# Hybrid attention, RG-LRU and PEER block on one core: more up products ahead, and every second down product in two float32r parts

## Chip, core and metric

One core of one Trainium2 chip runs the whole program. The metric is device time in microseconds, the median of several runs. TensorE (PE) multiplies, VectorE (DVE), ScalarE (ACT) and GpSimd (POOL) work on tiles in on-chip memory, SyncE (SP) issues most transfers; GpSimd issues the gathers by index.

## What is computed

512 tokens of width 1024 go through one layer: RMSNorm, one projection that feeds differential attention (8 heads, block-causal) and an RG-LRU branch, a gated merge, an output projection, and then a PEER layer, which is what the change is about. PEER picks for each token, in each of 8 heads, 16 of 16384 experts by product keys, that is 128 experts a token, and adds up

```
u = u_tab[idx]                                  # (token, head, 16, 1024)
act = gelu(einsum('thkd,td->thk', u, hb))
wts = softmax(top_s) * act
out = einsum('thk,thkd->td', wts, v_tab[idx])
```

All in float32.

## The kernel before, in words

Token blocks are numbered 0 to 3, 128 tokens each. A first pass (`p0`) takes block 0 through attention, RG-LRU and merge, a second pass (`p1`) blocks 1 to 3, its matmuls in two float32r parts (a value is a high part and a rest, and a product is three matmuls: high by high, high by low, low by high; helper `mm`, lines 206 to 211). PEER is done in two ways. For blocks 0 and 1 `experts` gathers the 128 picked rows of u and v of each token (1 MB for one slot of 128 tokens, an indirect DMA on GpSimd's queue) and VectorE does two passes over each: a dot product (line 855) and an accumulation into x1 (line 838). For blocks 2 and 3 (256 tokens) the work is dense: all 16384 experts, in 128 chunks of 128.

The dense part of a chunk c is an *up* product (tokens by the chunk's 128 rows of u, 8 accumulated products of 256 columns into PSUM, then gelu to an output y), a weight table (how much each token wants each expert), and a *down* product (y times table gives o; o times the chunk's rows of v is accumulated over all chunks in PSUM tile `acc`, 4 products of 512 columns).

Stages, in order of time, after the second pass's key products (`p1.keys`, whose last matmul is at 940 us):

1. Top-k on VectorE for blocks 1 to 3. Beside it, `ups_far` runs `LEAD` = 26 up products ("far", PSUM tile `pup`).
2. `wbuild`, 16 groups of 16 tokens: the table is built by one-hot products (PSUM tile `pw`) from one-hots that VectorE, ScalarE and GpSimd make, and is stored to DRAM (`w_d`) group by group; tiles of 12 chunks of it are loaded back (`wload`), the last two groups' rows only after the last store. 13 more up products (`up_near`, PSUM tile `st`) belong to this stage, seven of them written inside the loop, six after it.
3. The loop over c from 0 to 127: `down(c)` for all, and from c = `HEAD` = 24 on one `up_near` a step until all 128 are made. The order `TURN` makes chunks 24 to 38 first, then 0 to 23, then 39 to 127.

The first `AHEAD` = 39 up products use plain float32 (the token side is tile `h2r`, one load of 512 KB of u each into one of three buffers `raw`). The 89 others split u into two float32r parts (`chunk`: ScalarE casts, line 899, VectorE subtracts, line 900) and take the token side from `h2T`, which the second pass's projection has left in two parts for all three blocks. The down product is plain float32: two instructions for each product. Tiles of v hold two chunks (1 MB).

A planner in the compiler simulates the program and fixes each engine's order and SyncE's order from it, mostly by the order of writing where several things are ready; a tile with n buffers makes the next user wait for the n-th last. Gathers are paced by hand: each step adds a share (`SHARE`: 0.2 for a far up, 0.5 for a group of the table, 0.6 for a down step, 1.1 for a step with both) and one expert slot is issued for each whole one, tied behind an instruction of that step. `trunk` holds pools of the attention part, which are given back after the second pass's projection; `mid` takes their place.

Of the kernel before, what the change touches and what calls it, by code (L numbers as in the profile page):

```python
# [9 lines left out]
F32 = mybir.dt.float32  # L10
F32R = mybir.dt.float32r
# [4 lines left out]
ALU = mybir.AluOpType  # L16
# [46 lines left out]
def block_kernel(  # L63
# [25 lines left out]
    pp = ctx.enter_context(tc.tile_pool(name="pp", bufs=2))  # L89
    dram = ctx.enter_context(tc.tile_pool(name="dram", bufs=1, space=bass.MemoryType.DRAM))  # L90
    wp = ctx.enter_context(tc.tile_pool(name="wp", bufs=4))
    ap = ctx.enter_context(tc.tile_pool(name="ap", bufs=1))
    rg = ctx.enter_context(tc.tile_pool(name="rg", bufs=5))
    trunk = ctx.enter_context(ExitStack())
    s4 = trunk.enter_context(tc.tile_pool(name="s4", bufs=2, side="right"))
    s2 = trunk.enter_context(tc.tile_pool(name="s2", bufs=5, side="right"))

# [107 lines left out]

    def mm(o, lhs, rhs, start, stop):
        terms = [(0, 0)] if len(lhs) == 1 or len(rhs) == 1 else [(0, 0), (0, 1), (1, 0)]
        for i, (a, b) in enumerate(terms):
            nc.tensor.matmul(  # L209
                o, lhs[a], rhs[b], start=start and i == 0, stop=stop and i == len(terms) - 1  # L210
            )


    in_turn = mybir.DependencyInfo(mybir.DependencyClass.Sync, mybir.DependencyReason.SCHED_ONLY)
# [597 lines left out]
    def run(*gens):  # L812
        gens = list(gens)
        while gens:
            for g_ in list(gens):
                try:
                    next(g_)
                except StopIteration:
                    gens.remove(g_)
# [60 lines left out]
    NG = NT2 // TG  # L880
    NCH = SLOTS

    HEAD, MID = 24, 15
    AHEAD = HEAD + MID

    TURN = list(range(HEAD, AHEAD)) + list(range(HEAD)) + list(range(AHEAD, SLOTS))

    LEAD = 26

    WI = 12  # L890

# [9 lines left out]
        return t[:, 0, :], t[:, 1, :]  # L901


    def up(c, S_):
        ks = lambda k: slice(k * P, (k + 1) * P)
        if c < AHEAD:
            u = wp.tile([P, D], F32, tag="raw", name=nm("u"), bufs=3)
            nc.sync.dma_start(u, u_t[c])
            for k in range(KT):
                mm(S_, [u[:, ks(k)]], [p1.h2r[:, k, :]], k == 0, k == KT - 1)  # L910
        else:
            uhi, ulo = chunk(u_t, c, "near")
            for k in range(KT):
                mm(S_, [uhi[:, ks(k)], ulo[:, ks(k)]], [h[:, k, P : 3 * P] for h in p1.h2T], k == 0, k == KT - 1)

    def gelu(o, S_):
        return A.activation(o, S_, AF.Gelu_apprx_tanh)  # L917
# [26 lines left out]


    def kept(c):
        if c >= HEAD:
            return mid.tile([P, NT2], F32, tag="ym", name=nm("y"), bufs=MID)
        if c % WI == 0:
            ybuf.append(rg.tile([P, WI, NT2], F32, tag="r", name=nm("ys")))  # L950
        return ybuf[-1][:, c % WI, :]
# [11 lines left out]

    def dense(ys, kT, kTb, stack):
        pool = lambda n, bufs=1, **kw: stack.enter_context(tc.tile_pool(name=n, bufs=bufs, reuse_waits="tile", **kw))
        dw = pool("dw")
        pa = pool("pa", space=PSUM)
        pt_ = pool("pt", 2, space=PSUM)
        acc = pa.tile([P, 2, D], F32, tag="acc", name="acc")

        def up_near():
            c = TURN[len(ys)]
            st = pt_.tile([P, 512], F32, tag="st", name=nm("st"))
            up(c, st[:, 0:NT2])
            y = kept(c)
            gelu(y, st[:, 0:NT2])
            ys[c] = y


        def wbuild(tg):  # L980
            o1s = wp.tile([P, TG, P], F32, tag="w8", name=nm("o1s"))
            st = wp.tile([P, NCH, TG], F32, tag="w8", name=nm("wst"))
            for t4 in range(0, TG, 4):
                pw = pt_.tile([P, 4, P], F32, tag="pw", name=nm("pw"))
                t0_ = tg * TG + t4
                o2 = dw.tile([P, 4, P], F32, tag="o2", name=nm("o2"), bufs=4)
                V.tensor_tensor(  # L987
                    o2, iota.unsqueeze(1).to_broadcast([P, 4, P]),
                    kTb[:, t0_ : t0_ + 4].unsqueeze(2).to_broadcast([P, 4, P]), op=ALU.is_equal,
                )  # L990
                for j in range(4):
                    t = t0_ + j
                    o1 = o1s[:, t4 + j, :]
                    k1, g1 = kT[:, 0, 0, t : t + 1], kT[:, 0, 1, t : t + 1]
                    if O1[j] == "A":

                        sq = dw.tile([P, P], F32, tag="osq", name=nm("osq"), bufs=2)
                        A.activation(sq, iota, AF.Square, bias=kT[:, 1, 0, t : t + 1])
                        A.activation(o1, sq, AF.Relu, scale=kT[:, 1, 1, t : t + 1], bias=g1)
                    else:  # L1000
                        e = nc.gpsimd if O1[j] == "P" else V
                        e.tensor_scalar(o1, iota, k1, g1, op0=ALU.is_equal, op1=ALU.mult)  # L1002
                    nc.tensor.matmul(pw[:, j, :], o2[:, j, :], o1, start=True, stop=True)  # L1003
                turn[0] = A.copy(st[:, :, t4 : t4 + 4], pw.rearrange("p t i -> p i t"))  # L1004
            nc.sync.dma_start(w_d[tg], st)

        ws, vs = [], []

# [9 lines left out]
        def down(c, y):  # L1018
            if c % WI == 0 and len(ws) * WI < NCH:
                wtile()  # L1020
                wload(len(ws) - 1)
            if c % 2 == 0:
                vs.append(wp.tile([P, 2, D], F32, tag="w8", name=nm("v")))
                nc.sync.dma_start(vs[-1], v_t[c : c + 2].rearrange("c p d -> p c d"))
            v_ = vs[-1][:, c % 2, :]
            o = mid.tile([P, NT2], F32, tag="o", name=nm("o"), bufs=OB)
            yv = y.rearrange("p (g t) -> p g t", g=NG)
            turn[0] = V.tensor_mul(o.rearrange("p (g t) -> p g t", g=NG), yv, ws[c // WI][:, :, c % WI, :])  # L1028
            for b in range(2):
                bs = slice(b * P, (b + 1) * P)  # L1030
                for hf in range(2):
                    hs = slice(hf * 512, hf * 512 + 512)
                    mm(acc[:, b, hs], [o[:, bs]], [v_[:, hs]], c == 0, c == NCH - 1)

        for tg in range(NG):
            wbuild(tg)
            share("w")
            if len(ys) < AHEAD - 6:
                up_near()

            if tg == 7:
                wtile()
                wload(0, 0, 8)
            elif tg == 13:
                wload(0, 8, 14)
        wload(0, 14, NG)
        while len(ys) < AHEAD:
            up_near()
        for c in range(NCH):
            down(c, ys[c])  # L1050
            if c >= HEAD and len(ys) < NCH:
# [20 lines left out]
    p1.rnn()  # L1072
    p1.merge()
    p1.project()
    trunk.close()
    mid = ctx.enter_context(tc.tile_pool(name="mid", bufs=1, reuse_waits="tile", side="right"))
    run(p1.keys())
    when = []
    for name, mark in marks:
        owed[0] += PACE[name]  # L1080
# [7 lines left out]
    def second():  # L1088
        x1 = cpool.tile([P, D], F32, tag="x1f", name="x1g")
        h2 = cpool.tile([P, D], F32, tag="h2f", name="h2g")  # L1090
        nc.sync.dma_start(x1, x1_d[0])
        nc.sync.dma_start(h2, h2_d)
        yield from experts(P, x1, h2, (p1.idx[:, 0, :], p1.g[:, 0, :]), lambda s: turn[0], True)

    ex = second()
    ys = ups_far(0, LEAD)
    p1.weights()
    kTs = picks_t()
# [86 lines left out]
```

## Time and profile before

| | us |
|---|---|
| median of 3 runs | 1912.57 |
| lowest, highest | 1909.86, 1913.16 |
| profiled execution | 1909.11 |
| its span | 1907.2 |
| PE, DVE, ACT, POOL busy | 1750.3, 1310.4, 783.9, 486.7 |
| up products, far (`pup`): first to last start | 940.5 to 1031.4 |
| one-hot products (`pw`): first to last start | 1051.9 to 1180.0 |
| down products (`acc`): first to last start | 1199.9 to 1900.0 |

Busy time of an engine counts its compute instructions. "Matmul" rows count machine instructions: a plain float32 product is two, a product of two-part operands three, a plain float32r one. Matmuls overlap at their ends, so the time of one is read best from a long chain of them.

### The profile page before, as it was taken

To read this page: it belongs to the slowest core of one execution; us is meant where nothing else is said; L and a number is where in the kernel's file an instruction comes from. 1 tells how busy PE (TensorE), PEld (TensorE's weight loads), DVE (VectorE), ACT (ScalarE), POOL (GpSimd) and SP (SyncE) were. 2 spreads that over 40 slices of the span, in tenths; PEclk is the share of its full clock that TensorE was granted. 3 is DMA by queue.
4 is the path that set the end of the run, shared out by engine and by line. 5 is a ranking of instruction groups with operands and counts; after the bars stand their busy time and mean duration, and the time that the engine had idled before them with its cause. 6 is when DMAs were issued, how large, how long until landed. Compare 5 with 4: busy or idle time off the path is not lost.

```text
span 1907.2 us, 25762 instructions
## 1 busy us (share of the span) xinstructions
PE 1750.3 (92%) x9166; PEld 1378.6 (72%) x9166; DVE 1310.4 (69%) x2818; ACT 783.9 (41%) x2193; POOL 486.7 (26%) x375
## 2 busy tenths in 40 slices
PE   7899898888798899989996985899999999999998
PEld 6789797778598677779985885347766767667763
DVE  2251387988889987689999567456666666666662
ACT  3382333767678754355311565012222322232220
POOL 1100001545322233342001466122222232222220
PEclk9899897889599899999998998899999999999999
DMA  7488454887877899987464577999999999999893
GB/s 296 149 279 309 172 193 162 297 293 283 308 274 278 313 389 357 386 305 271 155 216 157 177 275 290 362 372 395 366 369 392 382 354 364 354 356 354 331 359 123
DMA packets 131471, 563.37 MB, mean 295 GB/s; under 512 B 11408, under 2 KB 43280, under 8 KB 88592
## 3 DMA queue, kind: packets, MB, share of 16 engines
q1 hardware_dynamic: 94480, 293.29, 42.8%
q0 software_dynamic: 36864, 268.45, 37.0%
q8 instruction: 72, 1.18, 0.2%
q14 instruction: 55, 0.45, 0.1%
HBM read 539.68 MB, written 22.02 MB: 295 GB/s over the span
## 4 chain that ended last, share of the span: by engine, by line
PE 71%; DVE 11%; DMA 9%; ACT 5%; issue 3%; POOL 1%; DVEq 0%; SPq 0%; ACTq 0%; POOLq 0%
PE acc L209 22%; PE st L209 16%; DMA uv<-in_uv_dram,idx 6%; PE ppq L209 5%; PE pkq L209 5%; PE pgt L209 4%; PE pbR L684 4%; PE pbA L677 3%; PE pwo L711 2%; DVE x1f L838 2%; PE pw L1003 2%; PE pvv L209 1%; DMA w_d<-wst 1%; DVE uv L855 1%; DMA v<-in_v_t_dram 1%
## 5 line engine op out<-in xcount | busy, mean ns | idle before, releaser
L848 POOL DMA_INDIRECT uv<-in_uv_dram,idx x256 | 360.4, 1408 | 1075.8 <-DVE x1g L838 284.3
L209 PE MATMUL acc<-v,o 128*128 128x512 f32 x1024 | 449.9, 595 | 22.2 <-DVE o L1028 19.6
L209 PEld LDWEIGHTS acc<-v,o 128*128 128x128 f32 x1024 | 191.8, 191 | 246.5 <-issue 223.3
L209 PE MATMUL st<-a,t 128*128 128x256 f32 x2136 | 282.2, 292 | 0.0
L209 PEld LDWEIGHTS st<-a,t 128*128 128x128 f32 x2136 | 262.5, 191 | 22.2 <-issue 18.9
L838 DVE SCALAR_TENSOR_TENSOR x1g<-uv,e,x1g 128x1024 f32<-128x1024 f32 x128 | 164.3, 1283 | 52.8 <-ACT e L861 52.8
L838 DVE SCALAR_TENSOR_TENSOR x1f<-uv,e,x1f 128x1024 f32<-128x1024 f32 x128 | 164.0, 1281 | 24.9 <-ACT e L870 24.8
L855 DVE SCALAR_TENSOR_TENSOR uv<-uv,h2f 128x1024 f32<-128x1024 f32 x128 | 156.0, 1220 | 34.5 <-DMA uv<-in_uv_dram,idx 27.9
L855 DVE SCALAR_TENSOR_TENSOR uv<-uv,h2g 128x1024 f32<-128x1024 f32 x128 | 155.9, 1218 | 19.4 <-DMA uv<-in_uv_dram,idx 19.4
L860 ACT ACTIVATE e<-e 128x1 f32<-128x1 f32 x128 | 25.8, 202 | 333.7 <-DVE uv L855 333.4
L900 DVE TENSOR_TENSOR t<-raw,t 128x1024 fp32r<-128x1024 f32 x89 | 108.9, 1223 | 68.7 <-ACT t L899 68.7
L1028 DVE TENSOR_TENSOR o<-y,w 128x256 f32<-128x256 f32 x104 | 44.0, 424 | 102.9 <-PE acc L209 102.9
L917 ACT ACTIVATE y<-st 128x256 f32<-128x256 f32 x89 | 34.2, 384 | 193.5 <-PE st L209 193.5
L230 DVE TENSOR_TENSOR wl<-raw,wh 128x1024 fp32r<-128x1024 f32 x76 | 90.8, 1218 | 19.0 <-ACT wh L229 7.3
L899 ACT CAST t<-raw 128x1024 fp32r<-128x1024 f32 x89 | 92.0, 1033 | 23.4 <-PE acc L209 23.4
L229 ACT CAST wh<-raw 128x1024 fp32r<-128x1024 f32 x76 | 76.7, 1046 | 35.0 <-PE pwo L711 12.3
L209 PE MATMUL pup<-r,u 128*128 128x256 f32 x416 | 90.4, 379 | 0.1
L209 PEld LDWEIGHTS pup<-r,u 128*128 128x128 f32 x416 | 78.8, 190 | 11.1 <-issue 0.5
L1003 PE MATMUL pw<-o1s,o 128*128 128x128 f32 x512 | 70.8, 295 | 15.0 <-DVE o L987 9.8
L1002 POOL TENSOR_SCALAR o1s<-iota,r 128x128 f32<-128x128 bf16 x64 | 74.2, 1168 | 38.3 <-ACT r L928 16.3
L1003 PEld LDWEIGHTS pw<-o1s,o 128*128 128x128 f32 x512 | 66.6, 206 | 20.0 <-ACT wst L1004 9.0
L209 PE MATMUL pkq<-wh,a 128*128 128x256 f32 x384 | 78.5, 298 | 0.0
(264 smaller groups left out, 3251.1 us busy)
## 6 DMA issues: line engine op xcount, KB each, us to landing
v<-in_v_t_dram SPq DMA_DIRECT2D x64, 1024.0 KB
raw<-in_u_t_dram SPq DMA_DIRECT2D x89, 512.0 KB
u<-in_u_t_dram SPq DMA_DIRECT2D x39, 512.0 KB
w<-in_w_br_dram SPq DMA_DIRECT2D x16, 1024.0 KB
w_d<-wst SPq DMA_DIRECT2D x16, 1024.0 KB
w<-w_d SPq DMA_DIRECT2D x9, 1536.0 KB
w<-in_w_qkv_dram SPq DMA_DIRECT2D x12, 1024.0 KB
raw<-in_w_qkv_dram SPq DMA_DIRECT2D x24, 512.0 KB
```

What stands on the lines that cost most here:

```text
L209: nc.tensor.matmul(o, lhs[a], rhs[b], start=start and i == 0, stop=stop and i == len(terms) - 1)
L229: A.copy(hi[:, i : i + 1024], raw)
L230: V.tensor_tensor(lo[:, i : i + 1024], raw, hi[:, i : i + 1024].bitcast(F32), op=ALU.subtract)
L677: nc.tensor.matmul(pb[:, 0:NT], w.raw(k * P, (k + 1) * P), self.aT[:, k, :], start=(k == 0), stop=(k == H - 1))
L684: nc.tensor.matmul(pb[:, 0:NT], w.raw(1024 + k * P, 1024 + (k + 1) * P), self.rnn_out(k, 1)[:, 0, :], start=(k == 0), stop=(k == NF - 1),)
L838: V.scalar_tensor_tensor(x1, v_, e_, x1, op0=ALU.mult, op1=ALU.add)
L848: i = nc.gpsimd.indirect_dma_start(out=t, out_offset=None, in_=uv, in_offset=bass.IndirectOffsetOnAxis(ap=idx[:, s : s + 1], axis=0),)
L855: i = V.scalar_tensor_tensor(t[:, 0:D], t[:, 0:D], 1.0, h2, op0=ALU.mult, op1=ALU.mult, accum_out=d)
L899: A.copy(t[:, 0, :], raw)
L900: V.tensor_tensor(t[:, 1, :], raw, t[:, 0, :].bitcast(F32), op=ALU.subtract)
L1002: e.tensor_scalar(o1, iota, k1, g1, op0=ALU.is_equal, op1=ALU.mult)
L1003: nc.tensor.matmul(pw[:, j, :], o2[:, j, :], o1, start=True, stop=True)
```

## The change

- `AHEAD` goes from 39 to 47 (8 more, in a new tile `spare`) and `LEAD` from 26 to 31: 31 far ups, 10 inside the build loop, and 6 after it (`HELD`). Those 6 get a dependency for order alone: the first matmul of each comes behind the last one-hot product.
- 81 up products are left for the loop over c. They take the token side from `h2s`, two float32r tiles made once from `h2r`.
- Every odd chunk's down product is done in two parts: v and o are each cast on ScalarE to float32r, the rest is a subtraction on VectorE, and `mm` makes three matmuls of each product. The parts' pool `sp` has one buffer a tile; it lies where the pool `dw` of the table build was.
- Pool `ap` (which holds `h2T`) moves into `trunk`, and `trunk` is closed after `p1.keys` rather than before.

```diff
--- before.py
+++ after.py
@@ -89,9 +89,9 @@
     pp = ctx.enter_context(tc.tile_pool(name="pp", bufs=2))
     dram = ctx.enter_context(tc.tile_pool(name="dram", bufs=1, space=bass.MemoryType.DRAM))
     wp = ctx.enter_context(tc.tile_pool(name="wp", bufs=4))
-    ap = ctx.enter_context(tc.tile_pool(name="ap", bufs=1))
     rg = ctx.enter_context(tc.tile_pool(name="rg", bufs=5))
     trunk = ctx.enter_context(ExitStack())
+    ap = trunk.enter_context(tc.tile_pool(name="ap", bufs=1, side="right"))
     s4 = trunk.enter_context(tc.tile_pool(name="s4", bufs=2, side="right"))
     s2 = trunk.enter_context(tc.tile_pool(name="s2", bufs=5, side="right"))
 
@@ -205,10 +205,13 @@
 
     def mm(o, lhs, rhs, start, stop):
         terms = [(0, 0)] if len(lhs) == 1 or len(rhs) == 1 else [(0, 0), (0, 1), (1, 0)]
-        for i, (a, b) in enumerate(terms):
+        made = [
             nc.tensor.matmul(
                 o, lhs[a], rhs[b], start=start and i == 0, stop=stop and i == len(terms) - 1
             )
+            for i, (a, b) in enumerate(terms)
+        ]
+        return made[0]
 
 
     in_turn = mybir.DependencyInfo(mybir.DependencyClass.Sync, mybir.DependencyReason.SCHED_ONLY)
@@ -880,12 +883,13 @@
     NG = NT2 // TG
     NCH = SLOTS
 
-    HEAD, MID = 24, 15
-    AHEAD = HEAD + MID
+
+    HEAD, MID, SPARE = 24, 15, 8
+    AHEAD = HEAD + MID + SPARE
 
     TURN = list(range(HEAD, AHEAD)) + list(range(HEAD)) + list(range(AHEAD, SLOTS))
 
-    LEAD = 26
+    LEAD, HELD = 31, 6
 
     WI = 12
 
@@ -901,17 +905,19 @@
         return t[:, 0, :], t[:, 1, :]
 
 
-    def up(c, S_):
+    def up(c, S_, after=None):
         ks = lambda k: slice(k * P, (k + 1) * P)
         if c < AHEAD:
             u = wp.tile([P, D], F32, tag="raw", name=nm("u"), bufs=3)
             nc.sync.dma_start(u, u_t[c])
             for k in range(KT):
-                mm(S_, [u[:, ks(k)]], [p1.h2r[:, k, :]], k == 0, k == KT - 1)
+                i = mm(S_, [u[:, ks(k)]], [p1.h2r[:, k, :]], k == 0, k == KT - 1)
+                if after is not None and k == 0:
+                    tc.add_manual_dep(i.ins, after.ins.name, in_turn, reason="in turn")
         else:
             uhi, ulo = chunk(u_t, c, "near")
             for k in range(KT):
-                mm(S_, [uhi[:, ks(k)], ulo[:, ks(k)]], [h[:, k, P : 3 * P] for h in p1.h2T], k == 0, k == KT - 1)
+                mm(S_, [uhi[:, ks(k)], ulo[:, ks(k)]], [h[:, k, :] for h in h2s], k == 0, k == KT - 1)
 
     def gelu(o, S_):
         return A.activation(o, S_, AF.Gelu_apprx_tanh)
@@ -944,6 +950,8 @@
 
 
     def kept(c):
+        if HEAD + MID <= c < AHEAD:
+            return spare[:, c - HEAD - MID, :]
         if c >= HEAD:
             return mid.tile([P, NT2], F32, tag="ym", name=nm("y"), bufs=MID)
         if c % WI == 0:
@@ -963,15 +971,16 @@
 
     def dense(ys, kT, kTb, stack):
         pool = lambda n, bufs=1, **kw: stack.enter_context(tc.tile_pool(name=n, bufs=bufs, reuse_waits="tile", **kw))
-        dw = pool("dw")
+        building = stack.enter_context(ExitStack())
+        dw = building.enter_context(tc.tile_pool(name="dw", bufs=1, reuse_waits="tile"))
         pa = pool("pa", space=PSUM)
         pt_ = pool("pt", 2, space=PSUM)
         acc = pa.tile([P, 2, D], F32, tag="acc", name="acc")
 
-        def up_near():
+        def up_near(after=None):
             c = TURN[len(ys)]
             st = pt_.tile([P, 512], F32, tag="st", name=nm("st"))
-            up(c, st[:, 0:NT2])
+            up(c, st[:, 0:NT2], after)
             y = kept(c)
             gelu(y, st[:, 0:NT2])
             ys[c] = y
@@ -1000,9 +1009,10 @@
                     else:
                         e = nc.gpsimd if O1[j] == "P" else V
                         e.tensor_scalar(o1, iota, k1, g1, op0=ALU.is_equal, op1=ALU.mult)
-                    nc.tensor.matmul(pw[:, j, :], o2[:, j, :], o1, start=True, stop=True)
+                    last = nc.tensor.matmul(pw[:, j, :], o2[:, j, :], o1, start=True, stop=True)
                 turn[0] = A.copy(st[:, :, t4 : t4 + 4], pw.rearrange("p t i -> p i t"))
             nc.sync.dma_start(w_d[tg], st)
+            return last
 
         ws, vs = [], []
 
@@ -1026,16 +1036,28 @@
             o = mid.tile([P, NT2], F32, tag="o", name=nm("o"), bufs=OB)
             yv = y.rearrange("p (g t) -> p g t", g=NG)
             turn[0] = V.tensor_mul(o.rearrange("p (g t) -> p g t", g=NG), yv, ws[c // WI][:, :, c % WI, :])
+            lhs, rhs = [o], [v_]
+            if c % 2:
+
+                vhl = sp.tile([P, 2, D], F32R, tag="vhl", name=nm("vhl"))
+                vhi, vlo = vhl[:, 0, :], vhl[:, 1, :]
+                A.copy(vhi, v_)
+                V.tensor_tensor(vlo, v_, vhi.bitcast(F32), op=ALU.subtract)
+                ohi = sp.tile([P, NT2], F32R, tag="ohi", name=nm("ohi"))
+                A.copy(ohi, o)
+                olo = sp.tile([P, NT2], F32R, tag="olo", name=nm("olo"))
+                V.tensor_tensor(olo, o, ohi.bitcast(F32), op=ALU.subtract)
+                lhs, rhs = [ohi, olo], [vhi, vlo]
             for b in range(2):
                 bs = slice(b * P, (b + 1) * P)
                 for hf in range(2):
                     hs = slice(hf * 512, hf * 512 + 512)
-                    mm(acc[:, b, hs], [o[:, bs]], [v_[:, hs]], c == 0, c == NCH - 1)
+                    mm(acc[:, b, hs], [t[:, bs] for t in lhs], [t[:, hs] for t in rhs], c == 0, c == NCH - 1)
 
         for tg in range(NG):
-            wbuild(tg)
+            last = wbuild(tg)
             share("w")
-            if len(ys) < AHEAD - 6:
+            if len(ys) < AHEAD - HELD:
                 up_near()
 
             if tg == 7:
@@ -1045,7 +1067,12 @@
                 wload(0, 8, 14)
         wload(0, 14, NG)
         while len(ys) < AHEAD:
-            up_near()
+            up_near(last)
+
+        A.copy(h2s[0], p1.h2r)
+        V.tensor_tensor(h2s[1], p1.h2r, h2s[0].bitcast(F32), op=ALU.subtract)
+        building.close()
+        sp = pool("sp")
         for c in range(NCH):
             down(c, ys[c])
             if c >= HEAD and len(ys) < NCH:
@@ -1072,9 +1099,9 @@
     p1.rnn()
     p1.merge()
     p1.project()
+    run(p1.keys())
     trunk.close()
     mid = ctx.enter_context(tc.tile_pool(name="mid", bufs=1, reuse_waits="tile", side="right"))
-    run(p1.keys())
     when = []
     for name, mark in marks:
         owed[0] += PACE[name]
@@ -1093,6 +1120,9 @@
         yield from experts(P, x1, h2, (p1.idx[:, 0, :], p1.g[:, 0, :]), lambda s: turn[0], True)
 
     ex = second()
+
+    h2s = [mid.tile([P, KT, NT2], F32R, tag=f"h{i}", name=f"h2s{i}") for i in range(2)]
+    spare = mid.tile([P, SPARE, NT2], F32, tag="spare", name="spare")
     ys = ups_far(0, LEAD)
     p1.weights()
     kTs = picks_t()
```

## Rows read from the trace of the kernel before

**Rows 1.** The page: busy times, slices of PE and DMA busy tenths, GB/s.

```profile
PE 1750.3 (92%) x9166; PEld 1378.6 (72%) x9166; DVE 1310.4 (69%) x2818; ACT 783.9 (41%) x2193; POOL 486.7 (26%) x375
...
PE   7899898888798899989996985899999999999998
...
DMA  7488454887877899987464577999999999999893
GB/s 296 149 279 309 172 193 162 297 293 283 308 274 278 313 389 357 386 305 271 155 216 157 177 275 290 362 372 395 366 369 392 382 354 364 354 356 354 331 359 123
```

**Rows 2.** Windows by stage (start:end, length, busy by engine, clock, DMA share, GB/s).

```profile
1031.40:1050.60 19.20, 1.21 (x5) 0.50 (x3) 19.06 (x78) 3.72 (x11) 4.42 (x4) 0.57 0.22 83
1051.00:1117.00 66.00, 65.73 (x391) 60.30 (x390) 34.89 (x82) 37.77 (x103) 26.14 (x26) 0.97 0.60 205
1117.00:1180.30 63.30, 48.60 (x333) 44.11 (x332) 53.36 (x123) 46.50 (x121) 53.00 (x41) 0.92 0.76 281
1180.30:1199.90 19.60, 0.02 (x1) 0.00 (x0) 2.96 (x5) 1.14 (x4) 1.43 (x1) 0.60 0.82 294
1200.00:1210.00 10.00, 10.00 (x18) 4.40 (x19) 2.60 (x5) 0.00 (x0) 1.87 (x2) 0.76 1.05 378
1210.00:1220.00 10.00, 10.00 (x24) 4.37 (x23) 5.79 (x9) 0.99 (x4) 1.87 (x2) 1.00 1.05 386
1200.00:1270.00 70.00, 67.44 (x151) 29.59 (x152) 30.80 (x48) 4.47 (x18) 15.88 (x12) 0.97 1.04 394
1300.00:1845.00 545.00, 545.00 (x2776) 380.33 (x2775) 366.06 (x463) 156.83 (x366) 138.79 (x96) 1.00 0.96 365
1440.00:1460.00 20.00, 20.00 (x102) 13.78 (x101) 14.61 (x20) 5.83 (x14) 5.97 (x4) 1.00 1.02 409
```

**Rows 3.** Chain of waits, 1300 to 1900 (start us, us, what).

```profile
1407.09 6.87 PE acc L209 x16
1413.95 5.75 PE st L209 x48
```

**Rows 4.** Waits of SyncE's queue, 1300 to 1850 (us in total, times, longest).

```profile
SPq L897 <- DVE t L900: 267.3, 63, 9.3
```

**Rows 5.** Chain of waits, 1030 to 1300.

```profile
1058.26 1.78 PE pw L1003 x16
1060.05 3.89 PE st L209 x18
...
1183.03 13.66 DMA w_d<-wst
```

**Rows 6.** Chain of waits, 858 to 960.

```profile
873.09 5.38 PE ppq L209 x31
...
945.92 14.25 PE pup L209 x66
```

**Rows 7.** Lines and forms, 1300 to 1850 (busy us, mean ns | idle before).

```profile
L838 DVE SCALAR_TENSOR_TENSOR x1g<-uv,e,x1g 128x1024 f32<-128x1024 f32 x98 | 125.6, 1281 | 44.3 <-ACT e L861 44.3
L855 DVE SCALAR_TENSOR_TENSOR uv<-uv,h2g 128x1024 f32<-128x1024 f32 x99 | 120.6, 1218 | 0.0
L900 DVE TENSOR_TENSOR t<-raw,t 128x1024 fp32r<-128x1024 f32 x85 | 104.0, 1223 | 63.7 <-ACT t L899 63.7
L899 ACT CAST t<-raw 128x1024 fp32r<-128x1024 f32 x85 | 87.8, 1033 | 17.1 <-PE acc L209 17.1
L1028 DVE TENSOR_TENSOR o<-y,w 128x256 f32<-128x256 f32 x87 | 36.8, 423 | 73.2 <-PE acc L209 73.2
L917 ACT ACTIVATE y<-st 128x256 f32<-128x256 f32 x88 | 33.8, 384 | 185.9 <-PE st L209 185.9
```

**Rows 8.** Waits of SyncE's queue, 1195 to 1300.

```profile
SPq L1016 <- DMA w_d<-wst: 13.2, 1, 13.2
```

**Rows 9.** Timeline of SyncE's queue, 1030 to 1300 (start us, us, xcount).

```profile
1196.70 0.88 SPq L1016 DMA_DIRECT2D w<-w_d  x2
```

**Rows 10.** Waits of PE, 1195 to 1300.

```profile
PE acc L209 <- DMA v<-in_v_t_dram: 2.6, 1, 2.6
```

## The prediction

> **What bounds the kernel now.** I read the page first: PE is busy 92% of the span and its last fourteen slices are nines but for the very last, and the DMA row reads eight or nine there too, at 331 to 395 GB/s [rows 1]. So two resources look full, and the next question is which of them the other waits for. The windows by stage answer that for each stretch [rows 2]: from 1300 to 1845 us, where every chunk has an up and a down product, PE is busy 545.00 of 545 us at clock 1.00, DVE 366.06 (67%), ACT 29%, DMA 365 GB/s. The chain of waits over the same stretch holds nothing but PE, in a pattern that repeats some 40 times: 16 acc instructions in 6.87 us, then 48 st instructions in 5.75 us [rows 3]. A pair of chunks costs 12.62 us, all PE. The SyncE queue meanwhile waited 267.3 us for buffers of u to come free [rows 4], so transfers were held back by the consumers and not by the DMA engines. This stretch is PE's.
>
> The stages before it are different. From 1031.4 to 1050.6 PE works 1.21 us of 19.2 and DVE 19.06: top-k on VectorE ends last, and PE has run out of up products [rows 2]. From 1051 to 1117 PE is full (65.73 of 66), alternating half a group of one-hot products (1.78 us) with one up product (3.89) [rows 2, 5]: the planner spent twelve of its thirteen up products here. From 1117 to 1180.3 PE is busy 48.60 of 63.3, POOL 53.00, DVE 53.36 [rows 2]. From 1180.3 to 1199.9 PE does nothing (0.02 us) [rows 2]: the last weight table goes out (13.66 us) and comes back before the first down product may start [rows 5], and the clock has fallen, so that 1200 to 1210 runs at a granted 0.76, part at 1.2 and part at 2.4 GHz, with 18 matmuls where the next window holds 24 [rows 2].
>
> **The change part by part.**
>
> *Up products ahead, 39 to 47.* Eight near up products leave the last stage. Each is 24 float32r matmuls of 256 columns at 5.75/48 = 119.8 ns [rows 3], 2.87 us; eight are **23.0 us** off a stretch where PE is the end. They come back as plain float32 products of 16 instructions at 14.25/66 = 216 ns [rows 6], 3.45 us each. Five go to the top-k stage: 17.3 us into 19.2 us where PE is idle beside DVE. What that stage pays is one more gathered expert (0.2 x 5), 1.28 + 1.22 us of DVE [rows 7], at worst 2.5 us; I take 1. Their loads cost nothing: 83 GB/s move there [rows 2].
>
> *Six tied behind the last one-hot product.* Six times 3.45 is 20.7 us of PE for the 19.6 us hole. Before, 13 near ups ran inside the build stage; now ten do. An up costs its pair 5.67 us in the PE-bound part, and half a group alone costs 63.3/20 = 3.2 us later, so three ups fewer end the build up to 7.5 us sooner; as the later part isn't PE's I take 5. Against it stands SyncE's queue: the load of the last weight rows sat there 13.2 us waiting for the store [rows 8] and went out at 1196.70 [rows 9], 16.4 us after the last one-hot product. The u tiles have three buffers, so three tied ups can have their data early; loads of the other three go out only as the first three are multiplied, and whichever the planner puts behind that weight load waits with it, and so do the v loads. If all three do: 16.4 + 3 us to land + 10.4 us of ups, start of the down products 10 us later than now. If none does: 1175.3 + 20.7 = 1196, 4 us earlier. I take 4 us of waiting: start unchanged, **0** (bounds -4 and +10). PE then comes warm to the down products: of ten us at clock 0.76 about 2.4 are won, **2** taken, 0 if it waits on loads.
>
> *Odd chunks in two float32r parts.* Now a down product is 8 instructions at 6.87/16 = 429.4 ns, 3.435 us [rows 3]. It becomes 12 float32r matmuls of 512 columns, which no row shows. Float32r takes 119.8 ns at 256 columns [rows 3] and 5.38/31 = 173.5 at 384 [rows 6]: 0.42 ns a column and 12 over, so 227 ns at 512 (an estimate; by proportion from 384 it would be 231), 2.73 us. The gain is 0.71 us an odd chunk, 64 of them: **45.5 us** at most, nothing at least if another engine takes over. Added for each: a cast of v on ACT (1.03 us) and of o (0.38), two subtractions on DVE (1.22 and 0.42), by the rows of the same shapes [rows 7].
>
> How much of the 45.5 stays, by stretch. *Middle, 81 steps, 40 odd, 28.4 us.* A pair then takes PE 11.91 us. DVE has 67% of 12.62 = 8.48 us a pair and gets 1.64: 10.1 of 11.91, 85%. DMA moves 4.67 MB a pair (u and v 0.52 each, 1.1 gathers of 1.05, 0.13 of table, twice): 370 GB/s now, 392 then; the fullest long stretch of the trace gave 394 over 70 us, and one of 20 us 409 [rows 2]. Both would be near their ends at once behind small rings of buffers, so I take 20 of 28.4. *First 24 steps, 8.5 us.* Here the trace is already at 394 GB/s and share 1.04 [rows 2], and PE already waited once for v (2.6 us) [rows 10]; faster PE asks for 0.52 + 0.6 x 1.05 + 0.13 MB in 3.08 us, 418 GB/s. 2 of 8.5. *Last 23 steps, 8.5 us.* Same demand as long as experts last (until about chunk 122 by the shares, before 118), and no ups to cover the split: its buffer is single, so cast and two subtractions, 2.87 us with o's, must fit in the 3.435 us of one even product, while DVE may be inside a 1.28 us expert step. 3 of 8.5. Sum **25** (bounds 0 and 45.5).
>
> *The rest.* The two parts of h2 (2048 columns a row: 2 us of ACT, 2.4 of DVE) come once, before the first near up, while 24 down products run: 0 (2.4 if they fell into top-k, where DVE has no cover). Moving the pools changes where tiles lie and that the far ups' outputs wait for the keys' last product, which is ahead of them on PE anyway: 0.
>
> **Sum.** On the profiled execution, 1909.1 us (its span of 1907.2 and 1.9 around it): -23 + 0 - 2 - 25 + 1 = -49, 1860. The median of the runs is 3.5 above the profiled one, so **1863**.
>
> The row shows 394 GB/s held over 70 us [rows 2]. The Trainium skill (DMA: Bandwidth & Descriptors, "Where 436 GB/s comes from") says that for HBM to SBUF a limit of about 358 GB/s per core binds. By that rule the last stage is at its end already, which is the third rival's time. The same page (section "Bandwidth") has 425 GB/s for large transfers with the neighbour core idle; by that 392 would pass. The trace's 394 lies between the two, and so the first doesn't hold here.
>
> **Rivals.**
> 1. *PE stays the end everywhere*, 0.15: all 45.5 us and the early start: 1909 - 23 - 4 - 2 - 45.5 + 1 = 1836, median 1839. For: PE was never late for anything in 545 us. Against: the first 24 steps at 394 GB/s.
> 2. *VectorE becomes the bound*, 0.15. DVE sat idle 63.7 us for ACT's half of the u split and 44.3 for the experts' scale [rows 7], 2.5 us a pair. If its fixed order keeps these, a pair takes 8.48 + 1.64 + 2.5 = 12.6 us, what it takes now, and only the moved ups pay, with 2 or 3 us from the ends: about 1884 to 1887. Against: such waits shrink as the engine waiting gets later.
> 3. *The DMA rate is a ceiling now*, 0.09. If 365 GB/s is all that this mix gives, the last stage is its bytes: only eight u tiles (4.2 MB, 11.5 us) leave, and the warm start 2: about 1899. For: share 0.96. Against: the buffers that SyncE waited for, and 394.
> 4. *Slower: the split starts too late*, 0.08. V's parts have one buffer and ACT and DVE work in order. If the cast of v stands behind a gelu that waits for the up just ahead (ACT waited 185.9 us for those [rows 7]), PE finds neither part when it comes to the odd product and waits 1.03 + 1.22 + 0.42 + the semaphores, 3 us. It decides from (23 + 2 + 45.5)/64 = 1.1 us an odd chunk; in half of the odd chunks it costs 96 and the result is 1912 - 70 + 96 = 1938. Against: between two odd products lie two ups and an even product, 9.2 us.
> 5. *The gains cancel*, 0.06: u loads late by 10 us, and both 2 and 3 in part: 1900 to 1912.
>
> The forecast (1850 to 1880) has 0.47. The range goes from rival 1 to rival 3: 1838 to 1900. Faster by over 0.2% (3.8 us, about what a measurement here tells from none): the forecast, rivals 1 to 3 and half of 5, 0.88; same 0.04; slower 0.08.
>
> **What would show it.** Float32r acc at 227 ns a start; six ups between the last one-hot product and the first acc, with less than 5 us of PE idle; 1200 to 1210 at clock 1.00; in the middle a pair at about 12.1 us, DVE near 83% and 385 GB/s; PE waits that name v's load in the first 24 chunks and the subtractions of v or o in the last 23. Wrong if PE waits for the parts in the middle, if acc in float32r is above 270 ns, or if the first down product starts after 1210.

## The result, and the profile after

The changed kernel takes 2120.16 us (median of 4 runs, 2117.3 to 2124.43), the kernel before beside it 1911.21 (1907.44 to 1913.16): ratio 1.1095, 95% interval 1.1067 to 1.1122. The forecast, 1863 with a range to 1900, missed by 257 us and had the sign wrong.

The page of the changed kernel, the lines that answer to [rows 1] and, in the last line, PE's slower group of down products (busy us, mean ns | idle before):

```profile
PE 1784.5 (84%) x9358; PEld 1447.8 (68%) x9358; DVE 1415.1 (67%) x2939; ACT 874.3 (41%) x2316; POOL 463.6 (22%) x375
...
PE   7899988887989998999997899985757667677788
...
PEclk9899989895999999899999899997878888888899
DMA  7587448876889998846567999996565565665575
GB/s 287 181 295 256 164 146 303 304 292 255 324 285 346 377 373 316 286 154 213 189 234 269 348 398 351 374 387 252 215 232 224 213 245 195 237 236 201 199 279 218
...
L209 PE MATMUL acc<-v,o 128*128 128x512 f32 x512 | 302.5, 745 | 181.6 <-DMA v<-in_v_t_dram 181.6
```

Up to slice 27 (which ends at 1428 us) PE and DMA look much as in the kernel before. From there on PE's nines are gone, the clock falls, and the DMA rate drops from over 350 to some 220 GB/s. Nothing is full there: the waits hang on one another in a circle. The windows place it (against [rows 2]):

```profile
1180.30:1199.90 19.60, 12.73 (x47) 10.46 (x46) 4.46 (x8) 2.05 (x6) 1.87 (x2) 0.74 1.03 390
1200.00:1210.00 10.00, 10.00 (x40) 7.14 (x39) 4.33 (x7) 1.76 (x6) 1.72 (x1) 1.00 0.83 314
...
1300.00:1400.00 100.00, 93.08 (x500) 70.69 (x499) 81.31 (x104) 38.70 (x82) 26.23 (x18) 1.00 1.00 388
1400.00:2000.00 600.00, 423.08 (x2008) 305.68 (x2008) 321.15 (x394) 158.45 (x322) 71.27 (x69) 0.84 0.62 232
```

The hole before the first down product is filled for the most part, and the granted clock behind it is 1.00. The loss is all behind 1400: PE 71% busy where it was 100%. Its waits from 1400 to 2040 (us in total, times, longest), and those of SyncE's queue:

```profile
PE acc L209 <- DMA v<-in_v_t_dram: 177.1, 30, 10.4
```

```profile
SPq L901 <- DVE t L904: 447.4, 56, 15.2
SPq L1034 <- PE st L209: 95.6, 32, 5.1
```

PE waits for v. V's load (L1034) waits for an up product (`st`) to give its buffer back, behind loads of u (L901) which wait longer still, for VectorE's part of u. Two timelines of the changed kernel show the circle, PE's and SyncE's queue's (start us, us; in brackets the idle time before):

```profile
1602.80 5.25 PE L209 MATMUL acc<-v,o 128*128 128x512 f32 x8 [4.29 <-DMA v<-in_v_t_dram]
...
1608.35 0.39 PE L209 MATMUL acc<-vhl,olo 128*128 128x512 f32 x1
...
1610.40 0.39 PE L209 MATMUL acc<-vhl,olo 128*128 128x512 f32 x1
1610.63 5.82 PE L209 MATMUL st<-h2s,t 128*128 128x256 f32 x48
1624.36 6.40 PE L209 MATMUL acc<-v,o 128*128 128x512 f32 x8 [7.91 <-DMA v<-in_v_t_dram]
...
1633.33 5.82 PE L209 MATMUL st<-h2s,t 128*128 128x256 f32 x48
```

```profile
1613.65 0.38 SPq L1034 DMA_DIRECT2D v<-in_v_t_dram  x1
1618.81 14.65 SPq L901 DMA_DIRECT2D raw<-in_u_t_dram  x2
1636.36 0.38 SPq L1034 DMA_DIRECT2D v<-in_v_t_dram  x1
```

Read it as a loop: the pair's first up starts at 1610.63 and gives its buffer back some 3 us later; v goes out at 1613.65; the down pair that needs it starts 10.7 us later, at 1624.36; it ends at 1633.33, and the next ups start. That is 22.7 us, and v goes out again after 22.7 us. Over the 30 pairs from 1413 us on, a turn takes 18.1 to 25.4 us, 20.3 on average. A pair cost 12.62 [rows 3]. The same place in the kernel before, PE and then SyncE's queue:

```profile
1608.50 7.03 PE L209 MATMUL acc<-v,o 128*128 128x512 f32 x16
1614.96 6.55 PE L209 MATMUL st<-a,t 128*128 128x256 f32 x50
1621.35 7.03 PE L209 MATMUL acc<-v,o 128*128 128x512 f32 x16
```

```profile
1603.61 0.73 SPq L1024 DMA_DIRECT2D v<-in_v_t_dram  x1
...
1615.79 0.38 SPq L1024 DMA_DIRECT2D v<-in_v_t_dram  x1
```

A v issued at 1603.61 can't be the one multiplied without a wait 4.9 us later, where v takes about 8 us to land (median 8.3 on the page after); it is for the pair at 1621.35. So the kernel before loads v one pair ahead, and the changed one no longer does: by the two traces v goes out 18.2 us (median of the pairs in the middle) before its down pair starts in the kernel before, and 8.4 in the changed one.

**Why.** Outputs of chunks 39 to 46 lie in `spare`, which is used once and returns nothing, while the ring `ym` still has 15 buffers. The up written at step 24 takes the buffer that step 24 frees when it makes o from y, and so on to step 38. The up written at step 39 finds the next buffer of the ring held by chunk 47, so its output can't be written before step 47, and every later up slips by up to eight steps: in PE's order the up products now stand a pair behind the down products where they stood a pair ahead (when chunk 74's down product starts, 91 up products have started in the trace before, where 89 are written ahead of it, and 95 in the trace after, where 97 are). The order of writing doesn't know of this. U's parts and v share four buffers (tag `w8`) and SyncE's in-order queue, and turns are given by the order of writing: an up written early but multiplied late holds a buffer and a place in the queue ahead of the v that is needed first.

### The profile page after: what moved, and what is told of

The parts are those of the page before. It is cut to its first block, busy times and chain, and to the rows that moved or that the text cites. A ratio compares the mean times of both kernels' runs of the same rounds, so it can differ in the third digit from the quotient of the medians.

```text
span 2115.5 us, 26476 instructions
## 1 busy us (share of the span) xinstructions
PE 1784.5 (84%) x9358; PEld 1447.8 (68%) x9358; DVE 1415.1 (67%) x2939; ACT 874.3 (41%) x2316; POOL 463.6 (22%) x375
## 5 line engine op out<-in xcount | busy, mean ns | idle before, releaser
L851 POOL DMA_INDIRECT uv<-in_uv_dram,idx x256 | 327.4, 1279 | 1345.6 <-DVE o L1038 631.1
L209 PE MATMUL acc<-v,o 128*128 128x512 f32 x512 | 302.5, 745 | 181.6 <-DMA v<-in_v_t_dram 181.6
L209 PEld LDWEIGHTS acc<-v,o 128*128 128x128 f32 x512 | 120.0, 244 | 322.7 <-DMA v<-in_v_t_dram 188.2
L209 PEld LDWEIGHTS st<-h2s,t 128*128 128x128 f32 x1944 | 236.0, 188 | 14.0 <-DVE t L904 3.7
L209 PE MATMUL st<-h2s,t 128*128 128x256 f32 x1944 | 239.5, 280 | 7.1 <-DVE t L904 3.1
L209 PE MATMUL acc<-vhl,ohi 128*128 128x512 f32 x512 | 185.6, 442 | 8.6 <-ACT vhl L1044 5.4
L209 PEld LDWEIGHTS acc<-vhl,ohi 128*128 128x128 f32 x512 | 97.3, 190 | 56.9 <-issue 26.3
L209 PE MATMUL pup<-r,u 128*128 128x256 f32 x496 | 107.6, 379 | 0.3 <-DMA u<-in_u_t_dram 0.3
L1045 DVE TENSOR_TENSOR vhl<-v,vhl 128x1024 fp32r<-128x1024 f32 x64 | 78.3, 1224 | 42.9 <-ACT vhl L1044 42.0
L233 DVE TENSOR_TENSOR wl<-raw,wh 128x1024 fp32r<-128x1024 f32 x76 | 90.6, 1216 | 17.7 <-PE pkq L209 6.6
L209 PE MATMUL acc<-vhl,olo 128*128 128x512 f32 x256 | 101.0, 394 | 0.0
## 6 DMA issues: line engine op xcount, KB each, us to landing
raw<-in_u_t_dram SPq DMA_DIRECT2D x81, 512.0 KB, 5.5
u<-in_u_t_dram SPq DMA_DIRECT2D x47, 512.0 KB, 4.0
raw<-in_w_qkv_dram SPq DMA_DIRECT2D x24, 512.0 KB, 5.9
```

The costliest lines, as they stand in the source:

```text
L209: nc.tensor.matmul(o, lhs[a], rhs[b], start=start and i == 0, stop=stop and i == len(terms) - 1)
L233: V.tensor_tensor(lo[:, i : i + 1024], raw, hi[:, i : i + 1024].bitcast(F32), op=ALU.subtract)
L851: i = nc.gpsimd.indirect_dma_start(out=t, out_offset=None, in_=uv, in_offset=bass.IndirectOffsetOnAxis(ap=idx[:, s : s + 1], axis=0),)
L1045: V.tensor_tensor(vlo, v_, vhi.bitcast(F32), op=ALU.subtract)
```

## The experiments

Each has the kernel before beside it (medians 1912.87, 1910.56, 1910.01 and 1912.76 us for the four sets). Intervals are of the ratio to it.

**One ring.** The eight outputs get eight more buffers of the ring; `spare` is gone.

```diff
-        if HEAD + MID <= c < AHEAD:
-            return spare[:, c - HEAD - MID, :]
...
-            return mid.tile([P, NT2], F32, tag="ym", name=nm("y"), bufs=MID)
+            return mid.tile([P, NT2], F32, tag="ym", name=nm("y"), bufs=MID + SPARE)
```

> The changed kernel with one edit: the eight outputs made further ahead are eight more buffers of the ring ym (23 instead of 15), not a tile of their own that is used once. Theory A (the ring): in the changed kernel output 62, written in step 39, needs the buffer of output 47, which chunk 47 gives back; the ups slip from one pair ahead of the down products to one behind, the u parts then get the shared w8 buffers before v does, and each load of v goes out only when the up just ahead of it is done. With 23 buffers nothing slips: PE waits for v under 20 us in all after 1400 us, a pair in the middle takes 12.0 to 12.4 us, total 1855 to 1890. Theory S (the split itself holds v's buffer too long, or comes too late): still above 2050.

1871.88 us (1869.05 to 1877.54), ratio 0.9798 [0.9763, 0.9834]: 248 us less than the changed kernel for the place of eight tiles. A window of it, PE's waits from 1200 to 1860, and the timeline of SyncE's queue:

```profile
1300.00:1800.00 500.00, 478.99 (x2665) 377.13 (x2664) 400.45 (x514) 196.43 (x418) 129.97 (x89) 0.99 0.98 371
```

```profile
PE st L209 <- DVE t L904: 15.1, 16, 2.4
PE st L209 <- ACT t L903: 5.9, 4, 1.5
PE acc L209 <- DMA v<-in_v_t_dram: 4.5, 1, 4.5
```

```profile
1611.02 0.39 SPq L1032 DMA_DIRECT2D v<-in_v_t_dram  x1
...
1623.32 0.38 SPq L1032 DMA_DIRECT2D v<-in_v_t_dram  x1
...
1635.90 0.64 SPq L1032 DMA_DIRECT2D v<-in_v_t_dram  x1
```

V goes out 12.3 and 12.6 us apart here, 12.6 on average in the middle, and PE waits for it once.

**No split, `spare` kept.** `if c % 2:` becomes `if False:`.

> The changed kernel with all down products in plain float32 (47 ups ahead, six tied, separate tile for the eight outputs kept). Theory A: the slip and the late v loads are still there, 2050 to 2150. Theory S: the loss is gone, 1880 to 1900.

2222.66 us, ratio 1.1623 [1.1562, 1.1684]; PE waited 139.3 us for v in the 400 us from 1400. The stall doesn't need the split; with the split the kernel is even 102 us faster. That is more than the 45.5 us by which the split shortens PE's work at full clock, and where the rest comes from isn't shown.

**One ring, no split** (both edits): the moved up products alone.

> Both edits: ring of 23 buffers and all down products in plain float32, so the moved ups alone. Theory A and S: 1880 to 1895 (23 us of near ups gone from the last stage, the start of the down products unchanged, 2 us of warm clock). If the moved ups buy nothing because the last stage is at its DMA rate: 1898 to 1910.

1882.68 us (1881.07 to 1888.38), ratio 0.9853 [0.9818, 0.9889]: 30 us faster than before.

**V in two buffers of its own, `spare` kept.** The first two v tiles are used in turn for all pairs; u's parts have the other two of the four.

```diff
-                vs.append(wp.tile([P, 2, D], F32, tag="w8", name=nm("v")))
+                if len(vs) < 2:
+                    vs.append(wp.tile([P, 2, D], F32, tag="w8", name=nm("v")))
+                else:
+                    vs.append(vs[-2])
```

> The changed kernel with v in two fixed buffers of its own (two of the four w8 buffers, used in turn), the tile for the eight outputs kept as in the change. The ups still slip by up to eight steps, but a part of u can't take v's buffer. Theory A, second link (the loss is the order in the shared buffers): PE hardly waits for v, 1860 to 1920. If the slip itself costs (the outputs wait in PSUM): above 2000.

1890.96 us (1890.09 to 1891.83), ratio 0.9888 [0.9848, 0.9929]: the outputs stay where the change put them, and 229 of the 248 us go. PE waited for v 26.1 us in all, 23.9 of it before 1400.

**Before, with outputs used once.** Nothing else of the change: of the 15 outputs in the ring of the kernel before, the last n go into a tile used once, and the ring has 15 - n.

```diff
-    HEAD, MID = 24, 15
+    HEAD, MID, SPARE = 24, 7, 8
...
+        if HEAD + MID <= c < AHEAD:
+            return spare[:, c - HEAD - MID, :]
```

> The kernel before, with one edit: of the 15 outputs kept ahead for chunks 24 to 38, the last eight lie in a tile that is used once, and the ring has seven buffers. No other part of the change. Theory A (a tile used once makes the later ups slip by its eight steps, and v's loads fall behind u's in the shared buffers): slow like the changed kernel, 2050 to 2250, with PE waiting for v from about chunk 32 on. If the slip needs the two-part products, the far ups or the tie: 1905 to 1920.

> The kernel before with the last 2 of its 15 outputs ahead in a tile that is used once, and a ring of 13 for the rest. Theory A (a used-once output makes the up products of the middle slip by one step for each such output; what costs is that u's loads get ahead of v's in the buffers that they share): a slip of two steps leaves the order of u's and v's loads as it is in the kernel before, so the time stays within 0.5% of 1911 us. Rival (any used-once output stalls the middle, in proportion to their number; eight cost 416 us): 416 x 2/8 = +104 us, about 2015.

> The same with the last 4 of the 15 in a tile used once and a ring of 11. Theory A: in the order of the loads, 16 of the 42 pairs from 15 to 56 have one more u load ahead of v, against 7 in the kernel before and 38 with eight used-once outputs, which cost 416 us: (16 - 7) / (38 - 7) x 416 = +121 us, about 2030, with v's loads late on TensorE in some pairs and not in others. Rival (in proportion to the number of such outputs): +208, about 2120. A loss under 20 us would say that the loss needs the whole slip of eight.

> The kernel before with the last 6 of its 15 outputs ahead in a tile used once and a ring of 9. In the written order of the loads a v stands behind three u loads instead of two in 37 of the pairs 15 to 56 (eight such outputs: 38, four: 16, two and none: 7). Theory (the loss sets in when that holds without a break, pair after pair, so that no pair in between lets SyncE's queue catch up): nearly all of the 416 us, 2250 to 2330. Rival (the loss goes with the slip of TensorE's order, and six steps are short of eight): 2000 to 2150, or under 1950 if only the full eight count.

The last two columns are counted in the traces: the up products started when chunk 74's down product starts (89 are written ahead of it), and how long v goes out before its pair starts (median of 26 pairs in the middle, us).

| used once | us | ratio, interval | ups | v ahead |
|---|---|---|---|---|
| none (the kernel before) | 1910.01 | 1 | 91 | 18.2 |
| 2 | 1909.18 | 1.0002 [0.9988, 1.0015] | 91 | 18.2 |
| 4 | 1915.53 | 1.0022 [1.0001, 1.0043] | 90 | 15.3 |
| 6 | 2112.18 | 1.1043 [1.095, 1.1136] | 88 | 9.1 |
| 8 | 2326.94 | 1.2178 [1.2154, 1.2203] | 86 | 7.5 |

One edit that changes no arithmetic makes the kernel before 22% slower. The loss is not in proportion to n, and the count of u loads ahead of v doesn't size it either: by it four should have cost 121 us and cost 5, and six should have cost nearly what eight cost and cost 200. The loss sets in where the ups fall behind their written place and v goes out hardly earlier than it takes to land (median 8.9 us on the page with six); with four it still goes out 15.3 us ahead. With eight, a window and PE's timeline:

```profile
1400.00:1600.00 200.00, 131.05 (x569) 85.14 (x567) 75.59 (x93) 34.33 (x74) 18.74 (x20) 0.80 0.57 204
```

```profile
1603.27 9.02 PE L209 MATMUL acc<-v,o 128*128 128x512 f32 x16 [8.74 <-DMA v<-in_v_t_dram]
1611.73 6.31 PE L209 MATMUL st<-a,t 128*128 128x256 f32 x48
1626.89 9.15 PE L209 MATMUL acc<-v,o 128*128 128x512 f32 x16 [8.86 <-DMA v<-in_v_t_dram]
```

With six, PE's waits and SyncE's queue's, 1400 to 1800:

```profile
PE acc L209 <- DMA v<-in_v_t_dram: 76.1, 22, 8.7
```

```profile
SPq L1026 <- PE acc L209: 155.6, 23, 10.1
```

There v's load waits for the last down product and not for an up, which fits a shorter loop (a pair takes 17.7 us on average, with eight 22.9). What sets these lengths, and the step between four and six, stays open.

**Eight used once, v in its own buffers**, on the kernel before (both edits above).

> The kernel before with the last 8 of its 15 outputs ahead in a tile used once (2326.9 us), and v in two buffers of its own, so that u's parts have the two others of the four to themselves. Theory (the loss is v's load behind u's in the shared buffers and the queue): the 416 us go but for the price of two buffers for u's parts, 1911 to 1950, and TensorE waits for v under 20 us in the last stage. Rival (the loss is TensorE's order itself, the up products a pair behind): above 2200.

1960.43 us (1957.91 to 1962.96), ratio 1.0249 [1.0192, 1.0307]: 366 of the 416 us go; 10 us above the range given, and PE waits for v 47.6 us in the last stage where under 20 was said. The timeline and a window show the middle:

```profile
1605.42 7.03 PE L209 MATMUL acc<-v,o 128*128 128x512 f32 x16
1611.88 6.31 PE L209 MATMUL st<-a,t 128*128 128x256 f32 x48
1618.03 7.03 PE L209 MATMUL acc<-v,o 128*128 128x512 f32 x16
```

```profile
1600.00:1800.00 200.00, 200.00 (x1020) 139.69 (x1019) 131.94 (x167) 58.86 (x132) 48.14 (x34) 1.00 0.92 354
```

A pair takes 12.61 us again with the up products still slipped. So there their later place costs nothing by itself; it costs through the buffers and the queue that v shares with them. What is left isn't the price of two buffers for u's parts, as I had expected: nearly all of PE's waiting is for v itself, before 1440. PE's waits from 1200 to 1440, then from 1440 to 2000:

```profile
PE acc L209 <- DMA v<-in_v_t_dram: 46.2, 7, 14.9
```

```profile
PE acc L209 <- DMA v<-in_v_t_dram: 1.3, 1, 1.3
```

In the first 24 steps, in which no up product runs, v could take all four buffers and now has two. It goes out as little as 6.7 us before its pair there; in the kernel before it was never under 20.4.

**The split by itself.** The changed kernel with the counts of before (39 ahead, 26 far, no tie, no `spare`).

> The changed kernel with the counts of before (39 ups ahead, 26 far, none tied, no tile used once): the two-part odd down products alone, with the h2 parts made from h2r. Theory A: nothing slips; from the difference of the ring kernel with and without the split (1872 and 1883) 1895 to 1908. By PE's count alone (45.5 us): 1866. If the split by itself is what hurts: above 1913.

1899.89 us (1896.56 to 1905.83), ratio 0.9946 [0.9926, 0.9965]: 11 us.

**The split in the middle alone**, in one ring: `if c % 2 and HEAD <= c < HEAD + NCH - AHEAD:`.

> The ring kernel with the two-part product only in odd chunks 25 to 103, where up products lie between; the 24 odd chunks at the two ends in plain float32. By PE's count 24 x 0.71 = 17 us slower than the ring kernel, 1889. If the two ends gain nothing, as I argued for most of it (transfers full in the first 24, no cover in the last): 1868 to 1877, the first 24 and the last 23 chunks as long as in the ring kernel within 4 us.

1891.21 us (1884.76 to 1891.94), ratio 0.9888 [0.9867, 0.991], against 0.9853 [0.9818, 0.9889] without any split and 0.9798 [0.9763, 0.9834] with all of it. No gain of the split in the middle alone shows; taking it away from the 24 odd chunks at the two ends costs 0.9%, 17 us (6 to 28 by the ends of the intervals). The profiled executions don't put all of that at the ends. Read from the starts of the down products (us, one ring each):

| split | first start | first 24 steps | middle 81 | last 23 |
|---|---|---|---|---|
| all | 1193.6 | 91.2 | 504.4 | 71.4 |
| middle | 1198.2 | 93.1 | 512.0 | 79.1 |
| none | 1199.5 | 88.4 | 506.7 | 79.1 |

Of the difference between the first two rows, 1.9 and 7.7 us lie where the split was taken away. The start and the middle differ too, so the edit moves other work as well; how isn't shown.

**Two buffers for o's parts**, one ring of 21 (45 ahead), and the same ring with one buffer each.

```diff
-                ohi = sp.tile([P, NT2], F32R, tag="ohi", name=nm("ohi"))
+                ohi = sp.tile([P, NT2], F32R, tag="ohi", name=nm("ohi"), bufs=2)
...
-                olo = sp.tile([P, NT2], F32R, tag="olo", name=nm("olo"))
+                olo = sp.tile([P, NT2], F32R, tag="olo", name=nm("olo"), bufs=2)
```

> The ring kernel with two buffers for o's high part and two for its rest, paid for by two outputs fewer ahead (45 instead of 47, ring of 21). Theory B (with one buffer ScalarE stands at the cast of o until the odd product before it is done, 114 us in all, and u's casts behind it come late, for which PE waits 21 us): PE's waits for u's parts fall below 8 us, total 1858 to 1870 in spite of two near ups more (+5.7 us). Theory C (VectorE at 80% or the transfers are the end): 1870 to 1882.

> The fastest version so far (45 up products ahead, all in one ring of 21, tied ups, split; the two float32r parts of o in two buffers each; 1853.6 us) with one buffer for each part, as in the changed kernel. Theory: the second buffers let VectorE make a step's parts while TensorE still reads the last ones, and are the cause of the gain against the ring of 23 with one buffer each (1871.9): then this one takes 1868 to 1880. Rival: the gain is that of two outputs fewer ahead (a ring of 21): then it takes 1850 to 1858.

With two buffers 1853.58 us (1849.87 to 1859.75), ratio 0.9712 [0.9685, 0.9738], the fastest version here, faster than both kernels; with one 1870.02 (1866.81 to 1878.1), ratio 0.9808 [0.9778, 0.9839]. So the second buffers are worth 16 us, and two outputs fewer ahead nothing that shows (1871.88 with the ring of 23). The version with two buffers first, then the one with one; of each the windows and then a row of PE's waits from 1200 to 1860:

```profile
1400.00:1500.00 100.00, 99.01 (x565) 78.07 (x565) 83.76 (x107) 40.98 (x88) 30.82 (x20) 1.00 1.02 401
...
1300.00:1800.00 500.00, 493.46 (x2750) 386.27 (x2749) 414.88 (x534) 201.01 (x429) 141.44 (x93) 1.00 0.99 383
```

```profile
PE st L209 <- DVE t L904: 7.2, 8, 0.9
```

```profile
1300.00:1800.00 500.00, 484.60 (x2719) 379.84 (x2718) 407.27 (x523) 200.36 (x426) 138.74 (x91) 1.00 0.99 377
```

```profile
PE st L209 <- DVE t L904: 13.5, 16, 0.9
```

PE gains 9 us in this window, and its waits are those of an up product for u's parts, not of a down product for its own parts. That fits a chain in which the single buffer holds back the o parts' cast and subtraction and, behind them in order, the parts of u; the chain itself was not tried. By chunks, the two profiled executions differ by 3.3 us in the start of the first down product (1190.7 against 1194.0), 2.6 in the first 24 steps, 11.5 in the middle 81 (488.5 against 500.0) and nothing in the last 23.

**Without the tie**, one ring of 23.

> 47 up products ahead in one ring of 23 with the split (1871.9 us), but without the tie that puts the last six of them behind the last one-hot product. Theory: the tie keeps the six beside the wait for w_d, where TensorE has nothing else (13.66 us before the first down product); without it they come earlier and that wait is empty: 5 to 13 us slower, 1877 to 1885. Rival: the order by loads puts them there in any case: within 3 us of 1871.9.

1877.23 us (1869.79 to 1882.71), ratio 0.9831 [0.9796, 0.9865] against 0.9798 [0.9763, 0.9834] with it: the intervals overlap, so its worth isn't settled by time. The hole is plain in the timelines: without the tie, with it in the same ring, and in the changed kernel:

```profile
1183.67 2.77 PE L1010 MATMUL pw<-o1s,o 128*128 128x128 f32 x22 [0.76 <-POOL o1s L1009]
1207.56 5.81 PE L209 MATMUL acc<-v,o 128*128 128x512 f32 x8 [21.13 <-DVE o L1036]
```

```profile
1184.89 8.90 PE L209 MATMUL st<-r,u 128*128 128x256 f32 x32 [6.75 <-DMA u<-in_u_t_dram]
1193.62 2.74 PE L209 MATMUL acc<-v,o 128*128 128x512 f32 x6
```

```profile
1173.36 10.53 PE L209 MATMUL st<-r,u 128*128 128x256 f32 x48
1190.76 9.90 PE L209 MATMUL st<-r,u 128*128 128x256 f32 x32 [6.87 <-DMA u<-in_u_t_dram]
1200.50 1.88 PE L209 MATMUL acc<-v,o 128*128 128x512 f32 x4
```

## Why the prediction was wrong, by its own steps

- **The step that failed** is the pair of 11.91 us in the middle (about 12.1 where 20 of the split's 28.4 us are kept). It takes over from the kernel before that v is always there in time, and so that "Eight near up products leave the last stage" while the other 81 keep their places. Where an output is kept decides when its buffer comes back, and so when a later up may run. "*The rest*" asks what moving the pools costs ("Moving the pools changes where tiles lie ... 0"); the new tile `spare`, which stood in the diff, has no term and no rival. What the runs showed in its place: a pair of 20.3 us on average, PE waiting 177.1 us for v, and 248 of the 257 us by which the forecast missed. With one ring the same change takes 1871.9.
- **That 1871.9 lies 9 above the forecast** is in part luck: the moved ups gave 6 us more than forecast and the split 14 less (the next points).
- **Eight ups fewer, warm clock, start:** -23, -2, +1 and 0 were forecast, 24 in all; one ring without split gives 30, interval 21 to 35. The start is at 1200.5 against 1199.9, as said, by terms that were each somewhat larger: the last one-hot product starts 6.8 us sooner (1173.2 against 1180.0; 5 was taken), and PE waits 6.87 us for u in the hole where under 5 was given. Five of the six tied ups come before the first down product, the sixth inside it. 1200 to 1210 runs at clock 1.00, as said (its 40 matmuls are not to be set against the 18 of [rows 2], as shorter ones are among them).
- **Float32r at 512 columns:** nine of them from 1608.35 to 1610.40 in the changed kernel, 228 ns each; the estimate was 227.
- **Where the split's 45.5 us stay:** 2 were forecast in the first 24 steps, 20 in the middle and 3 in the last 23, 25 in all, over double what came (11). By the table above, all against none, the middle gains 2.3 and the last 23 steps 7.7; the first 24 gain nothing inside the stretch, 3.1 with the earlier start. So the middle was much too high and the last stretch too low. In the middle a pair took 12.45 us with one ring where about 12.1 was said. I had VectorE at 85% (it came to 400.45 of 500 us, 80%), but counted busy time and not the order behind single buffers; with the second ones 16 us come back, and the middle then looks as forecast: a pair of 12.06 us, VectorE 83%, 383 GB/s.
- **Rival 2** (a pair of 12.6 us) came nearest in the middle; its cause, VectorE's waits for the u split and the experts, wasn't tried. **Rival 3** (the DMA rate) falls for the middle: 401 GB/s over 100 us with PE 99% busy. By the Trainium skill (DMA: Bandwidth & Descriptors, "Where 436 GB/s comes from") about 358 GB/s per core binds; this trace doesn't agree. For the first 24 steps, where the split gained nothing inside the stretch, a limit by the DMA rate isn't refuted. **Rival 4**, the slower one, named v but the wrong wait: not its parts but its load.
- **Slips in the sums,** none of which moves the forecast: the cast of v and the two subtractions are 2.67 us by the rows (3.05 with the cast of o), not 2.87; the bound of +10 for the start leaves out the 5 us of the shorter build, with which it is +5; the chances of faster add up to 0.89.

## What to carry to other kernels

Before costing work that is moved ahead, follow each of its buffers: which instruction gives it back, and which later step was living on that return. Buffers used once are a hole in the ring behind them: here later users slipped by up to as many steps as there were such buffers, which cost 5 us for four and 416 for eight. Where two streams share a pool and an in-order queue, count for each how many steps ahead its load goes out before and after the change; a stream that goes from one pair ahead to none puts the transfer's time to land into every turn of the loop.

## What was not expected of the hardware

- A wait cost twice here. With PE 66% busy (eight outputs used once) the granted clock was 0.80, and 16 matmuls of a down pair took 9.02 to 9.15 us instead of 7.03: 2 us a pair on top of 8.8 of waiting. The first of them, from 1603.3 to 1612, ran at a granted clock of 0.78, after a wait in which it was 0.66.
- The DMA engines moved 401 GB/s over 100 us beside PE at 99.01 of 100 us (two buffers for o's parts); before the change the rows have 394 over 70 us and 409 over 20 [rows 2].
